# A hybrid encoder step in strassen form on one core: the first of the activations' sums, made by VectorE next to its second term

## The chip, the core and the metric

The kernel runs on one core of a Trainium2 chip. A core has five engines with a queue each: TensorE (PE; its weight loads are shown as PEld), VectorE (DVE), ScalarE (ACT), GpSimd (POOL) and SyncE (SP), which issues most transfers. Every engine takes its instructions in the order in which the program wrote them; between engines they wait on semaphores. The metric is the device time in microseconds (us) of one execution. All times here are of one profiled execution unless another source is named.

## The reference

One layer of an encoder runs over 2048 prompt frames and 64 frames of a running stream (17 tiles of 128 rows, the last of 64). What matters here is its second half:

```
def _post(x, mix, ln1_g, ln1_b, w_gate_up, w_down, ln2_g, ln2_b):
    h = _layernorm(ALPHA * x + mix, ln1_g, ln1_b)
    gu = h @ w_gate_up
    f = (jax.nn.silu(gu[..., :D_FF]) * gu[..., D_FF:]) @ w_down
    return _layernorm(ALPHA * h + f, ln2_g, ln2_b)
```

`h` has 1024 features, `D_FF` is 2816 = 22 slices of 128. Ahead of it stand a projection, a windowed attention, a gated mixer and an output projection, which take the first 600 us or so and are not touched.

## The kernel before

Numbers are float32. A product keeps that precision by splitting each operand into a rounded high part (`hi`, a cast by ACT) and the rest (`lo`, a subtraction by DVE, sometimes by POOL), and by three matmuls: hi·hi, hi·lo, lo·hi.

The second half goes over the tokens in four blocks (`b` = 0 to 3, of 576, 512, 512 and 512 tokens). In a block, each slice `i` of the 22 of gate and up is computed with Strassen's scheme in seven products (numbers 1 to 7) of 12 matmuls over 256 columns, in the order 1, [4 and 3 of the slice before], 5, 6, 2, 7. `product` issues one and then what evacuates its bank: ACT copies it into a buffer of the tag `tmp` (L915), DVE adds a bank to such a buffer (L919, L946), ACT takes the silu (L950, L958), and `out` multiplies gate by up (L926) into the activations `g`, with `sh` = 0 and 1 for the two halves of the block's tokens.

For two slices together (a pair `c` = slices 2c and 2c+1) the down projection is also done in seven products, in 23 pairs: c = 2 to 9 in blocks 1 and 2, and c = 2 to 8 in block 3 (`strassen`). The four quarters of the pair's activations are x = `g` of the even slice and y = `g` of the odd slice, each with the token halves 0 and 1. Products 1, 2 and 4 take x[0], y[0] and y[1] as they are (`put_f` splits them at once). Products 5, 6, 7 and 3 take sums: s5 = x[1] + y[1], s6 = s5 - x[0], s7 = x[0] - x[1], s3 = y[0] - s6. `f_sums` makes these four, `put_hi` casts one into a half of a buffer `ff` (L886) and `put_lo` subtracts (L890). `unit` does one down product for one tile of rows: three matmuls over 512 columns, hi·hi (L1333), hi·lo (L1334) and lo·hi (L1335, the only one that reads the lo part of the activations), and DVE adds the bank to `y` (L1338).

The order is written out by hand. The gate and up products of all blocks form one list; after the product at a position, what `todo` holds for this position is issued in the order in which it was entered. For a pair, p0 is the position of product 3 of its odd slice, where its last activations come out. Position p0+1 is product 5 of the next slice, p0+2 its 6, p0+3 its 2, p0+4 its 7, p0+5 product 1 of the slice after, p0+6 and p0+7 products 4 and 3. Units: 1 at p0 and p0+2, 2 at p0+1 and p0+3, 5 at p0+5 and p0+7, 6 at p0+6, and so on. The weights of the units are cast and subtracted by `split_hi` (L1322) and `split_lo` (L1326): those of product 5 at p0+2 and p0+3, those of 6 at p0+3 and p0+4. In blocks 1 and 2, POOL also makes eight differences of `h` for the next block (L747), at positions that fall into the pairs c = 3 and c = 5. The splits of the gate and up weights `wf` are shared by ACT (cast, L112) and DVE or POOL (subtraction, L113).

Of the kernel before, what the change touches and what calls it, by code (L numbers as in the profile page):

```python
# [11 lines left out]
ALU = mybir.AluOpType  # L12
# [33 lines left out]
def hybrid_step(ctx: ExitStack, tc: tile.TileContext, x_prompt, x_sample, xT_prompt, xT_sample, cache_kT, cache_v, w_in,  # L46
                ln_v_g, ln_v_b, sinks, w_spatialT, vecs, w_out, w_gate_up, w_down, ln2_g, ln2_b, rope,
                y_prompt, y_sample, wk_p, wv_p, nk_s, nv_s, nvm_s):
    nc = tc.nc
# [794 lines left out]
    ffs, spare, g_t, f_sum = {}, [], {}, {}  # L844
# [26 lines left out]
        f = ffs[b, c, prod] = half_form()  # L871
        split(f[:, 0], f[:, 1], src)

    def f_sums(b, c):

        x, y = g_t.pop((b, 2 * c)), g_t.pop((b, 2 * c + 1))
        for prod, o, a, d, op in ((5, y[:, 1], x[:, 1], y[:, 1], ALU.add), (7, x[:, 1], x[:, 0], x[:, 1], ALU.subtract),
                                  (6, x[:, 0], y[:, 1], x[:, 0], ALU.subtract), (3, y[:, 0], y[:, 0], x[:, 0], ALU.subtract)):
            nc.gpsimd.tensor_tensor(out=o, in0=a, in1=d, op=op)
        for prod, o in ((5, y[:, 1]), (6, x[:, 0]), (7, x[:, 1]), (3, y[:, 0])):  # L880
            f_sum[b, c, prod] = o

    def put_hi(b, c, prod):

# [12 lines left out]
    def product(b, i, prod):  # L897
        n = TB[b] // 2
        w, h = wf.pop((b, i, prod)), forms[b, prod]
        bk = {1: "A", 6: "A", 7: "A", 4: "A", 2: "B", 5: "C", 3: "C"}[prod]  # L900
        new = prod in (1, 2, 5)
        if new:
            acc[i, bk] = (bank({"A": f"A{i % 2}", "C": f"C{i % 2}", "B": "S1"}[bk]) if b else
                          ps1.tile([P, 512], F32, name=f"acc{bk}", tag="x", bufs=6))
        ps = acc[i, bk][:, :n]
        for k in range(4):
            wh, wl, hh, hl = w[:, 0, k], w[:, 1, k], h[:, 0, k, :n], h[:, 1, k, :n]

            nc.tensor.matmul(ps, wh, hh, start=(new and k == 0), stop=False, skip_group_check=not new)  # L909
            nc.tensor.matmul(ps, wh, hl, start=False, stop=False, skip_group_check=not new)  # L910
            nc.tensor.matmul(ps, wl, hh, start=False, stop=(k == 3), skip_group_check=not new)  # L911

        def keep(key):
            part[i, key] = tmp(key)
            nc.scalar.copy(part[i, key][:, :n], ps)  # L915

        def add(key, to):
            part[i, key] = a = part.pop((i, to))
            nc.vector.tensor_tensor(out=a[:, :n], in0=ps, in1=a[:, :n], op=ALU.add)  # L919

        def out(sh, g, u):
            if strassen(b, i):
                if sh == 0:
                    g_t[b, i] = f2.tile([P, 4, P], F32, name="g", tag="wsum", bufs=3).rearrange("p (s a) q -> p s (a q)", s=2)
                to = g_t[b, i][:, sh]
                nc.vector.tensor_tensor(out=to, in0=u, in1=g, op=ALU.mult)  # L926

                if not (sh and i % 2 == 0):
                    put_f(b, i // 2, 4 if sh else 1 + i % 2, to)
                if sh and i % 2:  # L930
                    f_sums(b, i // 2)
                return
            nc.vector.tensor_tensor(out=g, in0=u, in1=g, op=ALU.mult)
            f = ff[b, i][:, :, sh * n:(sh + 1) * n] if b == 0 else half_form()
            if b:
                ff[b, i, sh] = f
            split(f[:, 0], f[:, 1], g)

        if prod == 1:
            keep("a0")  # L940
        elif prod == 6:
            keep("a1")
        elif prod == 7:
            keep("a2")
            part[i, "c22"] = a = part.pop((i, "a2"))
            nc.vector.tensor_tensor(out=a[:, :n], in0=acc[i, "C"][:, :n], in1=a[:, :n], op=ALU.add)  # L946
        elif prod == 2:
            add("c11", "a0")
            g = part[i, "c11"][:, :n]
            nc.scalar.activation(g, g, AF.Silu)  # L950
        elif prod == 4:
            if b == 0:
                ff[b, i] = f2.tile([P, 4 * NHX], F32R, name="ff", tag="ff", bufs=4)[:, :4 * n].rearrange("p (s t) -> p s t", s=2)
            out(0, part.pop((i, "c11"))[:, :n], ps)
        elif prod == 3:
            add("c12", "a1")
            g = part.pop((i, "c12"))[:, :n]
            nc.scalar.activation(g, g, AF.Silu)  # L958
            out(1, g, part.pop((i, "c22"))[:, :n])
# [32 lines left out]
    for t in range(2, NP):  # L992
        a = t - 1
# [459 lines left out]
    for b in range(NB):  # L1453
        first, last = b * NO, b == NB - 1
        for c in range(NFF // 2):
            p0 = start[b, 2 * c + 1, 3]
            d_load, d_split = (-8, -1, -5, -3), (-3, 5, -1, 4)
            if strassen(b, 2 * c):
                for prod, q0, q1 in ((1, -6, -3), (2, -5, -2), (5, -2, 2), (6, -1, 3), (3, 1, 5), (7, 4, 7), (4, 6, 9)):
                    at(p0 + q0, lambda b=b, c=c, prod=prod: load_f(b, c, prod))  # L1460
                    at(p0 + q1, lambda b=b, c=c, prod=prod: split_hi(b, c, prod))
                    at(p0 + q1 + 1, lambda b=b, c=c, prod=prod: split_lo(b, c, prod))
                for q, prod, u in ((0, 1, 0), (1, 2, 0), (2, 1, 1), (3, 2, 1), (5, 5, 0), (6, 6, 0), (7, 5, 1), (8, 3, 0), (8, 6, 1),
                                   (9, 3, 1), (10, 7, 0), (11, 7, 1), (12, 4, 0), (13, 4, 1)):
                    at(p0 + q, lambda b=b, c=c, prod=prod, u=u: unit(b, c, prod, u))
                for q, prod in ((3, 5), (4, 6), (5, 3), (6, 7)):
                    at(p0 + q, lambda b=b, c=c, prod=prod: put_hi(b, c, prod))
                    at(p0 + q + 1, lambda b=b, c=c, prod=prod: put_lo(b, c, prod))
                continue
            if b == 0:  # L1470
                d_load, d_split = (-6, -2, 8, 0), (1, 0, 10, 3)
                for j, q0, q1 in ((0, 2, 4), (1, 4, 6), (2, 5, 7), (3, 11, 13)):
                    at(p0 + q0, lambda c=c, j=j: w_sum(c, j))
                    at(p0 + q1, lambda c=c, j=j: w_store(c, j))
            elif c == 0:
                d_load, d_split = (-5, 1, -3, 2), (0, 6, 3, 7)
            elif c == 1:
                d_load, d_split = (-8, -1, -4, 1), (-3, 5, 1, 6)
            elif c == NFF // 2 - 1 and not last:
                d_load, d_split = (0, 2, 1, 6), (5, 7, 6, 9)  # L1480
            elif last and c == NFF // 2 - 2:
                d_load, d_split = (-7, -5, -6, -2), (-4, -2, -3, 2)
            if last and c == NFF // 2 - 1:
                d_load, d_split = (-14, -11, -13, -8), (-11, -3, -4, -2)
            for h in range(2):
                for i in (2 * c, 2 * c + 1):
                    at(p0 + d_load[2 * (i % 2) + h], lambda b=b, i=i, h=h: load_d(b, i, h))
                    at(p0 + d_split[2 * (i % 2) + h], lambda b=b, i=i, h=h: split_d(b, i, h, b == NB - 1 and i > NFF - 3 and (i, h) != (NFF - 2, 0)))
            if c < NFF // 2 - (2 if last else 1):
                where = (5, 6, 7, 8, 9, 12, 13, 14, 15, 16) if b == 0 else (2, 4, 5, 7, 9, 10, 12, 13)  # L1490
                if c == 0 and b:
                    where = (10, 12, 14, 16, 17, 18, 19, 19) if b == 1 else (6, 10, 12, 14, 15, 16, 17, 18)
                for k, (h, t) in enumerate((h, t) for h in (range(2) if b else (1, 0)) for t in TILES[b]):
                    at(p0 + where[k], lambda b=b, c=c, t=t, h=h: down(b, c, t, h))
            elif not last:
                new = list(TILES[b + 1])
                if b:
                    at(p0 + 3, lambda t=new.pop(0): new_y(t))
                late = 0 if b else 2
                for k, t in enumerate(TILES[b]):  # L1500
                    for h in range(2):
                        at(p0 + 10 + 2 * k + (h if b else 2 - h), lambda b=b, c=c, t=t, h=h: down(b, c, t, h))
                    steps = finish_steps(t)
                    for q, f in zip((11, 12, 13, 15, 17), steps):
                        at(p0 + 2 * k + q + late, f)
                    at(p0 + 2 * k + 20 + late, lambda t=new.pop(0): new_y(t)) if new else None
        if not last:
            for pos, f in later_steps(b + 1):
                at(first + NO + pos, f)
    for pos in range(EARLY, len(order)):  # L1510
        b, i, p = order[pos]
# [102 lines left out]
```

## Time and profile before

| | |
|---|---|
| time, median of 3 runs | 2208.36 us (2204.99 to 2209.4) |
| the profiled execution's own time | 2207.18 us |
| its span, first to last instruction | 2205.4 us |
| mean granted TensorE clock | 0.987 of full speed |
| PE busy | 2089.7 us, 95% |
| DVE busy | 1640.3 us, 74% |
| ACT busy | 997.0 us, 45% |
| POOL busy | 702.2 us, 32% |

A profile of this kind has a page (engines, the span in slices, the chain of waits, groups of instructions) and views that are asked for: a list of who waited for whom, a timeline of one engine, and busy times by window. In a timeline a row gives the start, the duration, the engine, the source line, the operation, what it writes and reads with shapes, and in square brackets the idle time of the engine ahead of it with the instruction that ended it. Durations of neighbours on an engine overlap a little, since instructions are pipelined.

### The profile page before, as it was taken

To read this page: it belongs to the slowest core of one execution; us is meant where nothing else is said; L and a number is where in the kernel's file an instruction comes from. 1 tells how busy PE (TensorE), PEld (TensorE's weight loads), DVE (VectorE), ACT (ScalarE), POOL (GpSimd) and SP (SyncE) were. 2 spreads that over 40 slices of the span, in tenths; PEclk is the share of its full clock that TensorE was granted. 3 is DMA by queue.
4 is the path that set the end of the run, shared out by engine and by line. 5 is a ranking of instruction groups with operands and counts; after the bars stand their busy time and mean duration, and the time that the engine had idled before them with its cause. 6 is when DMAs were issued, how large, how long until landed. Compare 5 with 4: busy or idle time off the path is not lost.

```text
span 2205.4 us, 36220 instructions
## 1 busy us (share of the span) xinstructions
PE 2089.7 (95%) x13081; PEld 1861.6 (84%) x13081; DVE 1640.3 (74%) x3176; ACT 997.0 (45%) x2385; POOL 702.2 (32%) x644
## 2 busy tenths in 40 slices
PE   8999999989989899999999999999999999999997
PEld 6888888867768799999888888888888888988986
DVE  6877777786788677777786776777677778577775
ACT  6666666563343444444433443453343444344443
POOL 0222222231132567666531332222243222122221
PEclk9999999989999999999999999999999999999999
DMA  5111111043554866676776767787587777767663
GB/s 196 39 39 39 39 39 39 27 159 118 196 193 172 306 231 235 247 285 241 273 278 240 257 238 277 264 285 278 199 287 273 251 257 276 257 225 262 242 230 121
DMA packets 189156, 447.22 MB, mean 203 GB/s; under 512 B 22608, under 2 KB 53072, under 8 KB 188976
## 3 DMA queue, kind: packets, MB, share of 16 engines
q1 hardware_dynamic: 168432, 426.22, 54.9%
q10 hardware_dynamic: 20368, 18.35, 2.5%
q8 instruction: 103, 1.69, 0.3%
q14 instruction: 77, 0.63, 0.1%
q0 software_dynamic: 176, 0.33, 0.0%
HBM read 345.94 MB, written 98.89 MB: 202 GB/s over the span
## 4 chain that ended last, share of the span: by engine, by line
PE 65%; DVE 20%; ACT 6%; DMA 4%; issue 3%; POOL 1%; ACTq 0%; SPq 0%; DVEq 0%; POOLq 0%
PE bankA L909 5%; PE bankA L911 4%; PE bankA L910 4%; PE pj L158 2%; PE pj L159 2%; PE pj L160 2%; PE bankC L910 2%; PE bankC L909 2%; PE bankC L911 2%; PE pd L159 2%; PE pd L160 2%; PE pd L158 2%; PE bankD L1334 2%; PE bankD L1333 2%; PE bankD L1335 2%
## 5 line engine op out<-in xcount | busy, mean ns | idle before, releaser
L113 POOL TENSOR_TENSOR wf<-guraw,wf 128x512 fp32r<-128x512 f32 x173 | 245.7, 1420 | 626.9 <-ACT wf L112 598.4
L909 PE MATMUL bankA<-hf,wf 128*128 128x256 f32 x1056 | 301.8, 286 | 12.2 <-ACT a L915 11.9
L910 PE MATMUL bankA<-hf,wf 128*128 128x256 f32 x1056 | 300.1, 284 | 0.0
L911 PE MATMUL bankA<-hf,wf 128*128 128x256 f32 x1056 | 299.9, 284 | 0.0
L909 PEld LDWEIGHTS bankA<-hf,wf 128*128 128x128 f32 x1056 | 201.4, 191 | 22.7 <-ACT a L915 14.6
L910 PEld LDWEIGHTS bankA<-hf,wf 128*128 128x128 f32 x1056 | 201.2, 191 | 9.1
L911 PEld LDWEIGHTS bankA<-hf,wf 128*128 128x128 f32 x1056 | 201.4, 191 | 0.0
L112 ACT CAST wf<-guraw 128x512 fp32r<-128x512 f32 x264 | 163.1, 618 | 19.7 <-DMA guraw<-in_w_gate_up_dram 12.6
L915 ACT COPY a<-bankA 128x256 f32<-128x256 f32 x198 | 73.5, 371 | 174.8 <-PE bankA L911 174.4
L910 PE MATMUL bankC<-hf,wf 128*128 128x256 f32 x528 | 149.4, 283 | 2.6 <-DVE hf L113 2.6
L909 PE MATMUL bankC<-hf,wf 128*128 128x256 f32 x528 | 149.8, 284 | 0.9 <-DMA wf<-wf_d 0.8
L911 PE MATMUL bankC<-hf,wf 128*128 128x256 f32 x528 | 148.5, 281 | 0.0
L1338 DVE TENSOR_TENSOR y<-bankD,y 128x512 f32<-128x512 f32 x184 | 125.6, 683 | 30.5 <-PE bankD L1335 30.5
L1326 DVE TENSOR_TENSOR wd<-draw,wd 128x512 fp32r<-128x512 f32 x161 | 130.8, 813 | 0.0
L950 ACT ACTIVATE a<-a 128x256 f32<-128x256 f32 (+1 forms) x88 | 37.4, 425 | 200.7 <-DVE a L919 199.7
L909 PE MATMUL accA<-hf,wf 128*128 128x288 f32 x352 | 105.2, 299 | 8.9 <-ACT a L915 5.3
L958 ACT ACTIVATE a<-a 128x256 f32<-128x256 f32 (+1 forms) x88 | 37.4, 424 | 155.9 <-DVE a L919 155.8
L910 PEld LDWEIGHTS bankC<-hf,wf 128*128 128x128 f32 x528 | 99.5, 188 | 8.6 <-DVE hf L113 3.2
L1338 DVE TENSOR_TENSOR y<-bankS,y 128x512 f32<-128x512 f32 x138 | 94.4, 684 | 16.1 <-PE bankS L1335 13.7
L909 PEld LDWEIGHTS bankC<-hf,wf 128*128 128x128 f32 x528 | 99.8, 189 | 7.0 <-DMA wf<-wf_d 1.4
L911 PE MATMUL accA<-hf,wf 128*128 128x288 f32 x352 | 104.1, 296 | 0.4 <-DVE wf L113 0.4
L910 PE MATMUL accA<-hf,wf 128*128 128x288 f32 x352 | 104.4, 297 | 0.0
(336 smaller groups left out, 6712.1 us busy)
## 6 DMA issues: line engine op xcount, KB each, us to landing
wf<-wf_d SPq DMA_DIRECT2D x264, 512.0 KB, 4.9
guraw<-in_w_gate_up_dram SPq DMA_DIRECT2D x110, 512.0 KB, 6.2
wf_d<-wf SPq DMA_DIRECT2D x88, 512.0 KB, 4.9
draw<-in_w_down_dram SPq DMA_DIRECT2D x153, 256.0 KB, 3.5
draw<-wt_d SPq DMA_DIRECT2D x92, 256.0 KB, 4.3
guraw<-in_w_gate_up_dram SPq DMA_DIRECT2D x66, 256.0 KB, 6.4
wt_d<-draw SPq DMA_DIRECT2D x44, 256.0 KB, 3.3
hraw<-h_d SPq DMA_DIRECT2D x42, 256.0 KB, 4.7
```

Of the source, the lines that this page charges most:

```text
L112: nc.scalar.copy(hi, src)
L113: (on or nc.vector).tensor_tensor(out=lo, in0=src, in1=hi.bitcast(F32), op=ALU.subtract)
L158: nc.tensor.matmul(out, ah, bh, start=(i == 0), stop=False)
L159: nc.tensor.matmul(out, ah, bl, start=False, stop=False)
L160: nc.tensor.matmul(out, al, bh, start=False, stop=(i == n - 1))
L909: nc.tensor.matmul(ps, wh, hh, start=(new and k == 0), stop=False, skip_group_check=not new)
L910: nc.tensor.matmul(ps, wh, hl, start=False, stop=False, skip_group_check=not new)
L911: nc.tensor.matmul(ps, wl, hh, start=False, stop=(k == 3), skip_group_check=not new)
L915: nc.scalar.copy(part[i, key][:, :n], ps)
L1326: nc.vector.tensor_tensor(out=hl[:, 1], in0=d_raw.pop((b, c, "f", prod)), in1=hl[:, 0].bitcast(F32), op=ALU.subtract)
L1333: nc.tensor.matmul(pd, fh, w[:, 0], start=new, stop=False, skip_group_check=not new)
L1338: nc.vector.tensor_tensor(out=y, in0=pd, in1=y, op=ALU.add)
```

## The change

POOL makes three sums in place of four. The first, s5, is made by DVE directly behind the multiplication that gives y[1], and written into the buffer `u`, which held the up factor of that multiplication. POOL's s6 reads it there. Cast and subtraction of s5 are issued a product earlier: `put_hi` at p0+2 in place of p0+3, `put_lo` at p0+3 in place of p0+4. In the changed program the line numbers are shifted: 918 for 919, 925 for 926, 914 for 915, 948 for 946, 885 for 886, 889 for 890, 952 for 950, 1324 for 1322, 1328 for 1326, 1340 for 1338; the new addition is line 928.

```diff
-    def f_sums(b, c):
+    def f_sums(b, c, first):
 
         x, y = g_t.pop((b, 2 * c)), g_t.pop((b, 2 * c + 1))
-        for prod, o, a, d, op in ((5, y[:, 1], x[:, 1], y[:, 1], ALU.add), (7, x[:, 1], x[:, 0], x[:, 1], ALU.subtract),
-                                  (6, x[:, 0], y[:, 1], x[:, 0], ALU.subtract), (3, y[:, 0], y[:, 0], x[:, 0], ALU.subtract)):
-            nc.gpsimd.tensor_tensor(out=o, in0=a, in1=d, op=op)
-        for prod, o in ((5, y[:, 1]), (6, x[:, 0]), (7, x[:, 1]), (3, y[:, 0])):
+        for prod, o, a, d in ((7, x[:, 1], x[:, 0], x[:, 1]), (6, x[:, 0], first, x[:, 0]), (3, y[:, 0], y[:, 0], x[:, 0])):
+            nc.gpsimd.tensor_tensor(out=o, in0=a, in1=d, op=ALU.subtract)
             f_sum[b, c, prod] = o
+        f_sum[b, c, 5] = first
...
                 nc.vector.tensor_tensor(out=to, in0=u, in1=g, op=ALU.mult)
+                if sh and i % 2:
+
+                    nc.vector.tensor_tensor(out=u, in0=g_t[b, i - 1][:, 1], in1=to, op=ALU.add)
 
                 if not (sh and i % 2 == 0):
                     put_f(b, i // 2, 4 if sh else 1 + i % 2, to)
                 if sh and i % 2:
-                    f_sums(b, i // 2)
+                    f_sums(b, i // 2, u)
                 return
...
-                for q, prod in ((3, 5), (4, 6), (5, 3), (6, 7)):
+                for q, prod in ((2, 5), (4, 6), (5, 3), (6, 7)):
                     at(p0 + q, lambda b=b, c=c, prod=prod: put_hi(b, c, prod))
                     at(p0 + q + 1, lambda b=b, c=c, prod=prod: put_lo(b, c, prod))
```

The first place is VectorE at p0 of the second pair of block 1 (c = 3). `a1_13492` is the gate after its silu, `a2_13541` the up factor, `g_13594` the odd slice's activations, `g_13413` the even slice's. Before:

```order
L926 TENSOR_TENSOR g_13594<-a2_13541,a1_13492 128x256
L113 TENSOR_TENSOR ff_13596<-g_13594,ff_13596 128x256
L1338 TENSOR_TENSOR y_12732<-bankD0_12798,y_12732 128x512
L113 TENSOR_TENSOR wf_13638<-guraw_13351,wf_13638 128x512
L1338 TENSOR_TENSOR y_12732<-bankS0_12902,y_12732 128x512
```

and with the change:

```order
L925 TENSOR_TENSOR g_13594<-a2_13541,a1_13492 128x256
L928 TENSOR_TENSOR a2_13541<-g_13413,g_13594 128x256
L113 TENSOR_TENSOR ff_13596<-g_13594,ff_13596 128x256
L1340 TENSOR_TENSOR y_12732<-bankD0_12798,y_12732 128x512
L113 TENSOR_TENSOR wf_13638<-guraw_13352,wf_13638 128x512
```

The addition stands between the multiplication and the subtraction for product 4; nothing else moves there.

The second place is VectorE from p0+3 to p0+5 of the same pair. `wd` are the units' weights (of product 5, then of 6), `a2_13724` the next slice's up factor; the rows of line 890 are the subtractions for products 5 and 6. Before:

```order
L919 TENSOR_TENSOR a0_13565<-bankS1_12228,a0_13565 128x256
L1326 TENSOR_TENSOR wd_13675<-draw_13574,wd_13675 128x512
L1338 TENSOR_TENSOR y_12778<-bankS0_12902,y_12778 128x512
L946 TENSOR_TENSOR a2_13724<-bankC0_12168,a2_13724 128x256
L1326 TENSOR_TENSOR wd_13698<-draw_13604,wd_13698 128x512
L890 TENSOR_TENSOR ff_13704<-g_13594,ff_13704 128x256
L1338 TENSOR_TENSOR y_12829<-bankS1_12228,y_12829 128x512
L890 TENSOR_TENSOR ff_13704<-g_13413,ff_13704 128x256
```

and with the change:

```order
L918 TENSOR_TENSOR a0_13565<-bankS1_12228,a0_13565 128x256
L1328 TENSOR_TENSOR wd_13675<-draw_13574,wd_13675 128x512
L1340 TENSOR_TENSOR y_12778<-bankS0_12902,y_12778 128x512
L889 TENSOR_TENSOR ff_13681<-a2_13541,ff_13681 128x256
L948 TENSOR_TENSOR a2_13725<-bankC0_12168,a2_13725 128x256
L1328 TENSOR_TENSOR wd_13700<-draw_13604,wd_13700 128x512
L1340 TENSOR_TENSOR y_12829<-bankS1_12228,y_12829 128x512
L889 TENSOR_TENSOR ff_13681<-g_13413,ff_13681 128x256
```

The subtraction for product 5 has moved ahead of two instructions, the addition of the up factor and the subtraction of product 6's weights. On ScalarE its cast moved likewise, from behind the cast of product 6's weights to ahead of the silu of p0+3.

## Rows read from the trace of the kernel before

**Rows 1.** The page's first part, the row of TensorE: busy time, share of the span, instructions.

```profile
PE 2089.7 (95%) x13081; PEld 1861.6 (84%) x13081; DVE 1640.3 (74%) x3176; ACT 997.0 (45%) x2385; POOL 702.2 (32%) x644
```

**Rows 2.** The list of waits of TensorE from 1195 to 2150 us, the stretch that holds the 23 pairs: who waited for whom, us in total, times, the longest.

```profile
PE bankS L1335 <- DVE ff L890: 25.3, 23, 2.2
PE bankS L909 <- DVE y L1338: 7.7, 6, 2.3
PE bankA L909 <- ACT a L915: 6.7, 3, 2.8
```

**Rows 3.** Timeline of TensorE at p0+5 and p0+6 of a pair of block 3 (c = 4), and the same wait one pair later.

```profile
2004.32 0.40 PE L1334 MATMUL bankS<-wd,ff 128*128 128x512 f32 x1
2005.77 0.50 PE L1335 MATMUL bankS<-wd,ff 128*128 128x512 f32 x1 [1.05 <-DVE ff L890]
2006.10 0.28 PE L909 MATMUL bankA<-hf,wf 128*128 128x256 f32 x1
...
2007.76 0.39 PE L1334 MATMUL bankD<-wd,ff 128*128 128x512 f32 x1
2007.99 0.40 PE L1335 MATMUL bankD<-wd,ff 128*128 128x512 f32 x1
...
2036.82 0.50 PE L1335 MATMUL bankS<-wd,ff 128*128 128x512 f32 x1 [1.05 <-DVE ff L890]
```

**Rows 4.** Timeline of VectorE in this pair, from the multiplication at p0 to the subtraction for product 6 at p0+5.

```profile
1996.35 0.43 DVE L926 TENSOR_TENSOR g<-a,a 128x256 f32<-128x256 f32 x1 [0.48 <-ACT a L958]
1997.25 0.43 DVE L113 TENSOR_TENSOR ff<-g,ff 128x256 fp32r<-128x256 f32 x1 [0.47 <-ACT ff L112]
1997.59 0.68 DVE L1338 TENSOR_TENSOR y<-bankD,y 128x512 f32<-128x512 f32 x1
1998.19 0.85 DVE L113 TENSOR_TENSOR wf<-guraw,wf 128x512 fp32r<-128x512 f32 x1
...
2000.74 0.42 DVE L919 TENSOR_TENSOR a<-bankS,a 128x256 f32<-128x256 f32 x1 [0.50 <-PE bankS L911]
2001.08 0.74 DVE L1326 TENSOR_TENSOR wd<-draw,wd 128x512 fp32r<-128x512 f32 x1
2001.75 0.68 DVE L1338 TENSOR_TENSOR y<-bankS,y 128x512 f32<-128x512 f32 x1
2003.27 0.42 DVE L946 TENSOR_TENSOR a<-bankC,a 128x256 f32<-128x256 f32 x1 [0.84 <-ACT a L915]
2003.61 0.68 DVE L1326 TENSOR_TENSOR wd<-draw,wd 128x512 fp32r<-128x512 f32 x1
2004.21 1.50 DVE L890 TENSOR_TENSOR ff<-g,ff 128x256 fp32r<-128x256 f32 x1
2006.30 0.69 DVE L1338 TENSOR_TENSOR y<-bankS,y 128x512 f32<-128x512 f32 x1 [0.59 <-PE bankS L1335]
2006.91 0.41 DVE L890 TENSOR_TENSOR ff<-g,ff 128x256 fp32r<-128x256 f32 x1
```

**Rows 5.** Timeline of GpSimd in this pair: the four sums, then a split of gate and up weights.

```profile
1997.76 3.52 POOL L879 TENSOR_TENSOR g<-g 128x256 f32<-128x256 f32 x4 [2.77 <-DVE ff L113]
2004.14 1.29 POOL L113 TENSOR_TENSOR wf<-guraw,wf 128x512 fp32r<-128x512 f32 x1 [2.86 <-ACT wf L112]
```

**Rows 6.** Timeline of ScalarE in this pair: the cast of product 5's weights, the silu of p0+3, the cast of s5, the copy at p0+4, the cast of s6, the cast that releases GpSimd's split.

```profile
1998.88 0.62 ACT L1322 CAST wd<-draw 128x512 fp32r<-128x512 f32 x1
2001.20 0.42 ACT L950 ACTIVATE a<-a 128x256 f32<-128x256 f32 x1 [1.69 <-DVE a L919]
...
2002.03 0.41 ACT L886 CAST ff<-g 128x256 fp32r<-128x256 f32 x1
2002.87 0.37 ACT L915 COPY a<-bankA 128x256 f32<-128x256 f32 x1 [0.43 <-PE bankA L911]
2003.13 0.41 ACT L886 CAST ff<-g 128x256 fp32r<-128x256 f32 x1
2003.44 0.62 ACT L112 CAST wf<-guraw 128x512 fp32r<-128x512 f32 x1
```

**Rows 7.** The raw gate and up weights of a slice: their issue on SP's queue in this pair (two transfers), the median time from issue to landing of the larger in the stretch 1990 to 2025 us, and the cast by ScalarE that reads them at p0+7.

```profile
1999.02 0.86 SPq L805 DMA_DIRECT2D guraw<-in_w_gate_up_dram  x2
...
guraw<-in_w_gate_up_dram SPq DMA_DIRECT2D x2, 512.0 KB, 6.2
...
2008.81 0.62 ACT L112 CAST wf<-guraw 128x512 fp32r<-128x512 f32 x1
```

**Rows 8.** Pair c = 3 of block 1, timelines of GpSimd, VectorE and TensorE: the second difference of `h`, the subtraction for product 6, and the matmul that reads it.

```profile
1256.62 1.48 POOL L747 TENSOR_TENSOR hsum<-hraw,hsum 128x512 f32<-128x512 f32 x1
...
1258.16 0.41 DVE L890 TENSOR_TENSOR ff<-g,ff 128x256 fp32r<-128x256 f32 x1
...
1259.26 0.40 PE L1335 MATMUL bankD<-wd,ff 128*128 128x512 f32 x1
```

**Rows 9.** Pairs c = 5 of blocks 1 and 2: ScalarE and TensorE waiting for transfers in block 1, the wait of block 2 in TensorE's timeline, and a window of block 2 behind it (busy us and instructions of PE, PEld, DVE, ACT and POOL, granted clock, DMA share, GB/s).

```profile
1322.59 0.62 ACT L1322 CAST wd<-draw 128x512 fp32r<-128x512 f32 x1 [3.79 <-DMA draw<-in_w_down_dram]
1323.85 0.39 PE L909 MATMUL bankC<-hf,wf 128*128 128x256 f32 x1 [0.78 <-DMA wf<-wf_d]
...
1681.46 0.50 PE L1335 MATMUL bankS<-wd,ff 128*128 128x512 f32 x1 [2.16 <-DVE ff L890]
...
1682.00:1685.00 3.00, 3.00 (x14) 2.90 (x14) 1.44 (x3) 0.21 (x2) 0.55 (x1) 0.50 1.04 421
```

## The prediction

> **What bounds the kernel now.** I read the page's engine row first: TensorE is busy for 95% of the span [rows 1], so only TensorE's idle time can be won, and the next view is the list of who ended it. In the stretch of the 23 pairs that list has one large entry: 25.3 us, 23 times, once in every pair. In each, the third matmul of a unit (L1335) waits for the subtraction that makes the lo part of a sum (L890). The next two entries, 7.7 and 6.7 us, have 9 waits between them [rows 2]. The timeline of TensorE gives the place: unit 5 at p0+5. Its second matmul starts at 2004.32, its third at 2005.77, and the next product's first at 2006.10 [rows 3]. At the pace of the next unit (second matmul at 2007.76, third at 2007.99, 0.23 us apart) the third would have started at 2004.55 or so and the next product 0.23 us behind it. The wait therefore moves everything behind it by 2006.10 - 2004.78 = 1.32 us, a little more than the 1.05 us of idle time in the list. It returns after 2036.82 - 2005.77 = 31.05 us, in the next pair [rows 3].
>
> Why the subtraction is late is in VectorE's timeline [rows 4]. At p0+4 it stands third: the addition of the up factor, which itself waits 0.84 us for ScalarE's copy, then the subtraction of product 6's weights, then the one for s5. That takes 1.50 us in place of the 0.41 us that the next one of its kind takes. GpSimd's split runs from 2004.14 to 2005.43 [rows 5], and VectorE's instruction, begun at 2004.21, ends at 2005.71, 0.28 us behind it. So two things delay TensorE: a place in the queue, and a collision with GpSimd at that place.
>
> **The move of cast and subtraction.** With the change the subtraction for s5 stands directly behind the addition to `y` that ends at 2001.75 + 0.68 = 2002.43, and in front of the addition at 2003.27. VectorE is idle there for 0.84 us [rows 4], the subtraction takes 0.41 us, and GpSimd has nothing between 2001.28 (1997.76 + 3.52) and 2004.14 [rows 5]. It ends near 2002.85, 1.7 us ahead of the 2004.55 at which TensorE wants it. The addition and the weights' subtraction behind it stay where they were, since their start is set by ScalarE's copy at 2002.87 [rows 6]; so the weights' subtraction still begins at 2003.61, ahead of GpSimd's split. The cast moves on ScalarE to behind the cast of 1998.88, which ends at 1999.50; ScalarE then has 1.69 us of idle time before the silu [rows 6], and the cast takes 0.41 us. Cost: nothing; without this cover it would delay the silu by at most 0.41 us.
>
> **The new addition.** 23 additions of 128x256 on VectorE at the 0.43 us of the multiplication beside them are 9.9 us of work. Each falls into the 0.47 us in which VectorE waits for the cast for product 4 anyway [rows 4]: the multiplication ends at 1996.78, the addition would end near 1997.25, and the subtraction behind it starts at 1997.25 now. I take 0. The bounds are 0 and, uncovered and passed on to TensorE in full, 9.9 us; a gain is excluded, since an instruction is added to that queue. Nearest to 0, because VectorE also idles 0.50 us at 2000.74 [rows 4].
>
> **What leaves GpSimd.** One of four sums goes, 3.52 / 4 = 0.88 us per pair, and the other three start at the addition's end (about 1997.3) instead of 1997.76, so the chain ends near 1997.3 + 2.64 = 1999.9 instead of 2001.28 [rows 5]. Nothing waits for it at the old time: the cast of s6 at 2003.13 stands behind ScalarE's copy of 2002.87 [rows 6]. Gain 0. The earlier start puts the sums beside the subtraction of 1997.25 and the `wf` subtraction of 1998.19, which may each lose up to one sum, 0.88 us. The idle 0.50 and 0.84 us behind them take up 1.34 us; I count nothing and keep 0.4 us per pair, 9 us, as the upper bound.
>
> *By the Trainium skill, page "SBUF — State Buffer", section "Who interferes with whom", a VectorE instruction with two SBUF inputs and a GpSimd instruction that reads SBUF block each other for the whole instruction, and the one issued first wins. The 1.50 us row agrees. By that rule the new addition is itself such an instruction, and it lets GpSimd go at the moment at which the subtraction for product 4 wants to start; this is the mechanism of the last rival below.*
>
> **What is late next.** TensorE's work behind p0+5 starts 1.32 us earlier, and what follows TensorE (copies, additions to `y`, products) follows it. Two things do not. The subtraction for s6 must be done for the third matmul of unit 6, now 2007.99, then 2006.67. It is behind the addition to `y` of unit 5, which moves from 2006.30 to 2004.98 and ends at 2005.67; GpSimd's split has ended at 2005.43; so the subtraction ends near 2006.05, with 0.6 us to spare. The raw weights are issued at 1999.02, land 6.2 us later at 2005.2, and are cast at 2008.81, then 2007.49 [rows 7]: 2.3 us to spare.
>
> **The sum.** 19 of the 23 pairs look like this one: 19 x 1.32 = 25.1 us. In the two pairs c = 3 GpSimd goes on from its split with a difference of `h`, 1256.62 to 1258.10. The subtraction for s6, now 1258.16, would be wanted by 1259.26 - 1.32 = 1257.94, but by the 0.28 us seen above it ends at 1258.38 [rows 8]. A wait of about 0.45 us, with 0.1 us of restart, stays: 2 x 0.75 = 1.5 us gained. In c = 5 of block 1 ScalarE waits 3.79 us and TensorE 0.78 us for transfers right behind [rows 9]; what is won is waited for there: 0. In c = 5 of block 2 the wait is 2.16 us, and behind it the granted clock is 0.50, TensorE's level of 1.2 GHz, for a window of 3 us, while transfers fill the queues (DMA share 1.04) [rows 9]. If all goes it is worth 1.32 + 1.11 + 1.5 = 3.9 us, if the transfers set the pace 0; I take 1.5. Together 25.1 + 1.5 + 0 + 1.5 = 28.1 us off the profiled execution's own 2207.18, which is 2179.1. The median shown is 1.2 us above that execution, so 2180.3; forecast 2180.
>
> **Rivals.** *The wait moves to unit 6.* If VectorE loses a race with GpSimd's split at p0+4 in ordinary pairs too, s6 is late as in c = 3: 0.75 instead of 1.32 us in each, 21 x 0.75 + 1.5 = 17.3 us, so 2191. For it: only 0.53 us lie between the weights' subtraction (2003.61) and the split (2004.14). Against: both are released by ScalarE's copies and keep their order.
>
> *The change does not reach TensorE.* The new cast could wait, for a half of an `ff` buffer or for the sum, or the transfers could give the saved time back everywhere. Then 2208. For it: c = 5. Against: ScalarE's 1.69 us, and 2.3 us of margin for the raw weights.
>
> *Slower: GpSimd wins at p0.* GpSimd's three sums start just as VectorE wants the subtraction for product 4. If GpSimd is first each time, four VectorE subtractions with both inputs in SBUF (product 4, `wf`, product 5's weights, s5) can each wait for a sum of 0.88 us: 3.5 us. The idle 0.47 (used by the addition), 0.50 and 0.84 us take 1.34 of it, and 2.2 us reach the additions that free banks S0 and S1. A wait of that length had the clock at 0.50 behind it in c = 5 [rows 9], worth 1.5 us more. It decides once the new wait passes 1.32 us; at 2.2 alone each pair loses 0.9 us and the time is 2208 + 19 = 2227. Against: three sums last 2.6 us and cannot meet four instructions spread over 5 us.
>
> **How the numbers follow.** Forecast 0.75, its own range 2175 to 2186: all of c = 5 won gives 2176, the addition half uncovered 2185. The wait at unit 6: 0.13. No effect: 0.06. Slower: 0.06. A difference under 0.2%, 4.4 us, could not be told from none, so faster 0.88, same 0.06, slower 0.06. The range for 8 in 10 reaches from 2174 to the second case with a little room for runs: 2194.
>
> **What would show it.** Right: the 23 waits for the subtraction of a sum at unit 5 are gone from TensorE's list, the period of ordinary pairs is 29.7 instead of 31.05 us, the subtraction for s5 takes 0.41 us, and VectorE's subtraction for product 4 still starts 0.9 us behind the multiplication. In the c = 3 pairs a short wait appears at unit 6. Wrong: waits at the third matmul of unit 6 in every pair, waits for additions to `y` at p0+3, or transfers ahead of the casts of raw weights.

## The result, and the profile after

The changed kernel is faster. The ratio of its time to that of the kernel before is 0.9872, with a 95% interval of 0.9844 to 0.9900; a second lot of runs of the same kernel gives 0.9863 (0.9849 to 0.9877). The median is 2181.45 us in the first lot (2178.54 us without one disturbed run of its four, which the ratio leaves out) and 2177.35 us in the second, against 2208.51 and 2207.32 us before. Forecast were 2180 us and a range of 2174 to 2194. The profiled execution took 2175.76 us, 31.4 us less than the one before.

The first view is again the list of waits of TensorE, from 1195 to 2150 us (the third matmul of a unit is now L1337, the first of a product L908).

```profile
PE bankS L908 <- DVE y L1340: 8.9, 7, 2.3
PE bankA L908 <- ACT a L914: 6.8, 5, 2.8
PE bankC L909 <- DVE hf L113: 2.1, 2, 1.0
PE bankD L1337 <- DVE ff L889: 1.7, 4, 0.7
PE bankS L1335 <- DVE y L1340: 0.4, 1, 0.4
```

The entry of 25.3 us and 23 times that led [rows 2] is gone. The entries for additions to `y` and ScalarE's copies, 7.7 and 6.7 us before, are 8.9 and 6.8. One entry has grown, from one wait to four: those at unit 6 (bank D, for the subtraction of s6), two of 0.19 us in the pairs c = 3 and two of 0.67 us in c = 5. Before it was this line:

```profile
PE bankD L1335 <- DVE ff L890: 0.3, 1, 0.3
```

The page's first row shows the same work in a shorter span, with one more VectorE and one fewer GpSimd instruction per pair:

```profile
PE 2082.2 (96%) x13081; PEld 1860.9 (86%) x13081; DVE 1624.5 (75%) x3199; ACT 997.5 (46%) x2385; POOL 691.3 (32%) x621
```

The timeline of TensorE at p0+5 of the pair of rows 3 (c = 4 of block 3):

```profile
1979.54 0.40 PE L1336 MATMUL bankS<-wd,ff 128*128 128x512 f32 x1
1979.77 0.39 PE L1337 MATMUL bankS<-wd,ff 128*128 128x512 f32 x1
1980.00 0.28 PE L908 MATMUL bankA<-hf,wf 128*128 128x256 f32 x1
```

Third matmul and next product follow at 0.23 us each; before, they came 1.45 and 0.33 us behind their neighbours [rows 3]. VectorE in this pair, the counterpart of [rows 4]:

```profile
1971.58 0.42 DVE L925 TENSOR_TENSOR g<-a,a 128x256 f32<-128x256 f32 x1 [0.48 <-ACT a L960]
1972.04 0.43 DVE L928 TENSOR_TENSOR a<-g 128x256 f32<-128x256 f32 x1
1972.48 0.43 DVE L113 TENSOR_TENSOR ff<-g,ff 128x256 fp32r<-128x256 f32 x1
...
1976.90 0.69 DVE L1340 TENSOR_TENSOR y<-bankS,y 128x512 f32<-128x512 f32 x1
1977.50 0.42 DVE L889 TENSOR_TENSOR ff<-a,ff 128x256 fp32r<-128x256 f32 x1
1978.49 0.42 DVE L948 TENSOR_TENSOR a<-bankC,a 128x256 f32<-128x256 f32 x1 [0.57 <-ACT a L914]
1978.83 0.68 DVE L1328 TENSOR_TENSOR wd<-draw,wd 128x512 fp32r<-128x512 f32 x1
1980.20 0.69 DVE L1340 TENSOR_TENSOR y<-bankS,y 128x512 f32<-128x512 f32 x1 [0.68 <-PE bankS L1337]
1980.81 0.41 DVE L889 TENSOR_TENSOR ff<-g,ff 128x256 fp32r<-128x256 f32 x1
```

The new addition (L928) runs from 1972.04 to 1972.47. The subtraction for product 4 starts at 1972.48, 0.90 us behind the multiplication, as before (1996.35 to 1997.25). The subtraction for s5 (L889) takes 0.42 us where it took 1.50, and ends at 1977.92, 1.85 us ahead of the matmul that reads it. GpSimd, the counterpart of [rows 5]:

```profile
1972.55 0.96 POOL L878 TENSOR_TENSOR g<-g 128x256 f32<-128x256 f32 x1 [2.33 <-DVE a L928]
1973.58 1.12 POOL L878 TENSOR_TENSOR g<-a,g 128x256 f32<-128x256 f32 x1
1974.78 0.74 POOL L878 TENSOR_TENSOR g<-g 128x256 f32<-128x256 f32 x1
1979.36 1.30 POOL L113 TENSOR_TENSOR wf<-guraw,wf 128x512 fp32r<-128x512 f32 x1 [3.84 <-ACT wf L112]
```

GpSimd's first sum starts 0.07 us behind VectorE's subtraction and takes 0.96 us, the second 1.12, the third, alone, 0.74. It is GpSimd that gives way at p0.

How the gain is spread shows when the starts of the multiplication at p0 (L926 before, L925 after) are taken from both timelines for all 23 pairs. Each line is the time from this multiplication in one pair to the one in the next, so it holds the wait at unit 5 of the pair named (20 such times, since the last pair of a block has none behind it):

```
pair                            before    after   changed kernel again (e4)
block 1, c = 2                   31.80    30.45    30.46
block 1, c = 3                   31.73    30.84    31.13
block 1, c = 4                   31.01    28.99    29.51
block 1, c = 5                   37.31    34.27    36.35
block 1, c = 6, 7, 8 (mean)      31.11    29.77    29.77
block 2, c = 2                   31.80    30.51    30.50
block 2, c = 3                   31.69    30.80    30.84
block 2, c = 4                   30.32    29.00    28.98
block 2, c = 5                   34.51    33.19    34.95
block 2, c = 6, 7, 8 (mean)      31.08    29.78    29.76
block 3, c = 2                   31.82    30.48    30.46
block 3, c = 3 to 7 (mean)       31.07    29.77    29.77
```

An ordinary pair loses 1.3 us, every time. The c = 3 pairs lose 0.89, and c = 4 and c = 5 are not alike from one execution to the next.

### The profile page after: what moved, and what is told of

The parts are those of the page before. It is cut to its first block, busy times and chain, and to the rows that moved or that the text cites. A ratio compares the mean times of both kernels' runs of the same rounds, so it can differ in the third digit from the quotient of the medians.

```text
span 2174.0 us, 36223 instructions
## 1 busy us (share of the span) xinstructions
PE 2082.2 (96%) x13081; PEld 1860.9 (86%) x13081; DVE 1624.5 (75%) x3199; ACT 997.5 (46%) x2385; POOL 691.3 (32%) x621
## 4 chain that ended last, share of the span: by engine, by line
PE 67%; DVE 19%; ACT 5%; DMA 4%; issue 3%; POOL 1%; SPq 0%; ACTq 0%; DVEq 0%; POOLq 0%
PE bankA L908 5%; PE bankA L909 5%; PE bankA L910 5%; PE pj L158 2%; PE pj L159 2%; PE pj L160 2%; PE bankC L909 2%; PE bankC L908 2%; PE bankC L910 2%; PE pd L159 2%; PE pd L160 2%; PE pd L158 2%; PE po L158 2%; PE po L160 2%; PE po L159 2%
## 5 line engine op out<-in xcount | busy, mean ns | idle before, releaser
L908 PE MATMUL bankA<-hf,wf 128*128 128x256 f32 x1056 | 301.5, 285 | 11.6 <-ACT a L914 11.5
L908 PEld LDWEIGHTS bankA<-hf,wf 128*128 128x128 f32 x1056 | 201.4, 191 | 23.4 <-ACT a L914 14.2
L908 PE MATMUL bankC<-hf,wf 128*128 128x256 f32 x528 | 149.4, 283 | 0.2
L908 PE MATMUL accA<-hf,wf 128*128 128x288 f32 x352 | 105.1, 299 | 8.9 <-ACT a L914 5.3
L908 PEld LDWEIGHTS bankC<-hf,wf 128*128 128x128 f32 x528 | 99.6, 189 | 5.7 <-ACT hf L112 0.5
```

## The experiments

Eleven kernels, in three lots. "Before" in a ratio is the kernel before, run on the same chip.

**e1, e2 and e3: which part of the change does it.** In e1 only the place changes; GpSimd makes all four sums as before:

```diff
-                for q, prod in ((3, 5), (4, 6), (5, 3), (6, 7)):
+                for q, prod in ((2, 5), (4, 6), (5, 3), (6, 7)):
```

> Only the place is changed: GpSimd still makes all four sums, cast and subtraction of s5 are issued a product earlier. Theory A (the place of the subtraction on VectorE is what counts, because the old place collides with GpSimd's split): GpSimd's first sum ends near 1998.5 in the pair of rows 4 to 6, a microsecond before ScalarE reaches the cast, so the 23 waits at unit 5 go as they do in the changed kernel; about 25 to 28 us faster than before, 2181 us, and some 2 to 4 us slower than the changed kernel, in the pairs c = 4 and c = 5 where GpSimd's chain is long. Theory B (the sum must be made by VectorE to be there in time): ScalarE waits for GpSimd, the waits at unit 5 stay at about 1 us, 2205 us or more.

Measured: ratio 0.9883 (0.9865 to 0.9900), median 2182.41 us. The waits at unit 5 are gone. VectorE's and ScalarE's rows in c = 4 of block 3:

```profile
1984.51 0.41 DVE L890 TENSOR_TENSOR ff<-g,ff 128x256 fp32r<-128x256 f32 x1
...
1981.57 0.41 ACT L886 CAST ff<-g 128x256 fp32r<-128x256 f32 x1
```

ScalarE casts the sum of GpSimd at once behind the weights' cast, without idle time, and the subtraction takes 0.41 us. Theory B falls: GpSimd's s5 is there in time. The 2 to 4 us that e1 was expected to lie behind the changed kernel can't be told from these ratios (0.9883 against 0.9872 and 0.9863, with intervals that overlap); e10 below settles it.

e2 is the opposite: VectorE makes the sum, cast and subtraction stay at p0+3 and p0+4 (the change without the line above).

> Only the maker is changed: VectorE makes s5, cast and subtraction stay at p0+3 and p0+4. Theory A: the subtraction still stands behind the weights' subtraction and meets GpSimd's split, so the 23 waits of 1.05 us stay; only the shorter chain of GpSimd can show, at most 4 us in the pairs c = 4 and c = 5; 2204 us (2202 to 2208). Theory B: the waits go, 2180 us.

Measured: ratio 0.9983 (0.9973 to 0.9994), median 2205.54 us. Its list of waits of TensorE from 1190 to 2150 us and its timeline of VectorE in block 3:

```profile
PE bankS L1337 <- DVE ff L889: 25.7, 23, 2.1
...
2002.32 1.50 DVE L889 TENSOR_TENSOR ff<-a,ff 128x256 fp32r<-128x256 f32 x1
```

All 23 waits are there, and the subtraction takes 1.50 us again, although its operand had been ready for 7.0 us (the addition ran from 1994.92 to 1995.34). The sum by VectorE alone gives 0.17%, some 4 us; its pairs c = 4 and c = 5 of block 1 took 30.31 and 33.99 us.

e3 leaves the sums and the casts as in the kernel before and exchanges two neighbours on VectorE at p0+4:

```diff
+                at(p0 + 4, lambda b=b, c=c: put_lo(b, c, 5))
                 for prod, q0, q1 in ((1, -6, -3), (2, -5, -2), (5, -2, 2), (6, -1, 3), (3, 1, 5), (7, 4, 7), (4, 6, 9)):
...
-                    at(p0 + q + 1, lambda b=b, c=c, prod=prod: put_lo(b, c, prod))
+                    if prod != 5:
+                        at(p0 + q + 1, lambda b=b, c=c, prod=prod: put_lo(b, c, prod))
```

> Before, with one exchange on VectorE at p0+4: the subtraction for s5 ahead of the subtraction of product 6's weights, all else as before. Theory A: the subtraction begins at 2003.6, half a microsecond ahead of GpSimd's split, takes 0.42 us and ends before TensorE wants it (2004.55): the waits go, about 25 us faster than before, 2182 us. If instead the length of VectorE's queue up to p0+4 were the cause, and not the collision, this moves the subtraction by 0.6 us only and about 0.7 us of each wait stays: 2197 us. A third outcome: the weights' subtraction now meets the split, and a wait of about 0.5 us appears at unit 6 in each pair: 2193 us.

Measured: ratio 0.9869 (0.9854 to 0.9884), median 2179.72 us: all of the gain. VectorE and GpSimd at p0+4 in block 3:

```profile
1983.16 0.42 DVE L890 TENSOR_TENSOR ff<-g,ff 128x256 fp32r<-128x256 f32 x1
1983.49 0.68 DVE L1326 TENSOR_TENSOR wd<-draw,wd 128x512 fp32r<-128x512 f32 x1
...
1983.69 1.65 POOL L113 TENSOR_TENSOR wf<-guraw,wf 128x512 fp32r<-128x512 f32 x1 [2.86 <-ACT wf L112]
```

The subtraction for s5 starts one instruction, some 0.6 us, sooner than in the order before and is done some 1.7 us sooner, because it no longer meets GpSimd's split. The weights' subtraction behind it is under way before the split starts, so VectorE loses nothing (0.68 us) and GpSimd takes 1.65 us instead of 1.29. A wait of 1.05 us that goes with a move of 0.6 us was a collision, not a long queue: at its old start, 2004.21, a subtraction of 0.42 us would have ended at 2004.63, 0.08 us behind the 2004.55 at which TensorE wanted it. The third outcome did not come either. In ordinary pairs the list has no wait for a subtraction; four short ones are left in the pairs c = 5, two at unit 5 (1.0 us in all) and two at unit 6 (1.5 us).

**e4: the changed kernel again.**

> The changed kernel once more, to see what repeats. If the gains per pair are the program's own, each ordinary pair again takes 29.8 us and the pairs c = 4 and c = 5 of block 1 together again about 63.3 us (28.99 + 34.27); if the 5 us won in those two pairs were an accident of the transfers, they move by some microseconds.

Measured: ratio 0.9863 (0.9849 to 0.9877). The profiled execution took 2181.13 us, 5.4 us more than the first one. The ordinary pairs are the same to 0.03 us (table above); c = 4 and c = 5 of block 1 take 65.86 us together instead of 63.26, and c = 5 of block 2 34.95 instead of 33.19. So the 5 us that the first profile showed as won in c = 4 and c = 5 of block 1 were half an accident. Most of what differs is TensorE's clock. In both pairs c = 5 of e4 there is a stretch with a granted clock near 0.50, the level of 1.2 GHz, and in the first profile of the changed kernel there is none. The windows of busy time (columns as in [rows 9]), first e4, then the first profile:

```profile
1332.00:1335.00 3.00, 3.00 (x15) 2.71 (x14) 1.71 (x3) 0.42 (x1) 0.00 (x0) 0.54 0.98 287
1680.00:1683.00 3.00, 2.95 (x14) 2.86 (x15) 1.53 (x3) 0.00 (x0) 0.00 (x0) 0.56 0.88 299
```
```profile
1330.00:1333.00 3.00, 3.00 (x22) 2.80 (x22) 1.86 (x4) 0.61 (x2) 0.00 (x0) 1.00 0.96 349
1676.00:1679.00 3.00, 3.00 (x24) 2.86 (x24) 2.52 (x5) 0.42 (x1) 0.00 (x0) 1.00 0.94 292
```

Added up over the pair, what the granted clock lacks of 1.00 comes to 1.7 us in each of the two pairs of e4 (an estimate from windows of 1 us). Without it they take 34.65 and 33.24 us, against 34.27 and 33.19.

**e5: the price of the addition.** The new line stands twice in the changed kernel:

```diff
                     nc.vector.tensor_tensor(out=u, in0=g_t[b, i - 1][:, 1], in1=to, op=ALU.add)
+                    nc.vector.tensor_tensor(out=u, in0=g_t[b, i - 1][:, 1], in1=to, op=ALU.add)
```

> The changed kernel with the new addition made twice (the second writes the same values again): 23 more instructions of 0.43 us on VectorE, not covered by the wait for ScalarE's cast, which the first one fills. Theory A (VectorE has slack at p0, 0.66 us of idle time before the bank of p0+3): no pair becomes longer, 2178 us as the changed kernel (2176 to 2182). Rival (VectorE is the bound next to TensorE, so each instruction more is paid): 23 x 0.43 = 9.9 us more, 2188 us.

Measured: ratio 0.9868 (0.9851 to 0.9884), median 2178.00 us, and 29.77 us for the ordinary pairs. VectorE in c = 4 of block 3:

```profile
1976.22 0.43 DVE L928 TENSOR_TENSOR a<-g 128x256 f32<-128x256 f32 x1
1976.69 0.42 DVE L929 TENSOR_TENSOR a<-g 128x256 f32<-128x256 f32 x1
1977.03 0.41 DVE L113 TENSOR_TENSOR ff<-g,ff 128x256 fp32r<-128x256 f32 x1
```

The second addition delays the subtraction for product 4 by 0.36 us, to 1.26 us behind the multiplication of 1975.77, and no ordinary pair pays for it. The idle time of VectorE ahead of p0+3 shrinks by the same 0.36 us, from 0.66 in the changed kernel to 0.30 in e5:

```profile
1975.96 0.42 DVE L918 TENSOR_TENSOR a<-bankS,a 128x256 f32<-128x256 f32 x1 [0.66 <-PE bankS L910]
```
```profile
1980.15 0.42 DVE L918 TENSOR_TENSOR a<-bankS,a 128x256 f32<-128x256 f32 x1 [0.30 <-PE bankS L910]
```

**e6: GpSimd's fourth sum put back.** The changed kernel with one more addition on GpSimd, whose result nobody uses:

```diff
+        nc.gpsimd.tensor_tensor(out=y[:, 1], in0=x[:, 1], in1=y[:, 1], op=ALU.add)
         for prod, o, a, d in ((7, x[:, 1], x[:, 0], x[:, 1]), (6, x[:, 0], first, x[:, 0]), (3, y[:, 0], y[:, 0], x[:, 0])):
```

> The changed kernel, but GpSimd also makes its old first addition (into the place where it stood, read by nobody), so its chain is as long as before. Theory A (GpSimd's shorter chain is worth nothing in ordinary pairs): ordinary pairs stay at 29.8 us; only c = 4 and c = 5 may grow, by up to 4 us together; 2178 to 2183 us. Rival (part of the gain comes from work taken off GpSimd): ordinary pairs grow by some tenths, 2185 us or more.

Measured: ratio 0.9876 (0.9861 to 0.9891), median 2180.02 us; ordinary pairs 29.77 us; c = 4 and c = 5 of block 1 29.00 and 34.74. Within what these pairs vary by, the fourth sum costs nothing that can be told.

**e7 and e8: what makes c = 5 long.** In e7 the loads, differences and stores for the next block move to other positions:

```diff
-            q = -100 + 24 * kk
+            q = -96 + 28 * kk
```

> The changed kernel with the differences of h for the next block (loads, subtractions on GpSimd, stores) put 4 positions later for the first half and 8 later for the second, so that they fall to p0+8 to p0+14 of the pairs c = 3 and c = 5. If the short waits left at unit 6 come from these subtractions, the c = 3 pairs go from 30.8 to 30.4 us and the waits at unit 6 go: 1 to 2 us, and up to 4 more if SP's queue is held for a shorter time in c = 5: 2173 to 2178 us. If not, no change in c = 3.

A miss: ratio 0.9902 (0.9886 to 0.9917), median 2185.63 us, slower than the changed kernel. The waits at unit 6 are gone from its list, but c = 3 takes 30.70 us in block 1, only 0.1 less, and 30.98 in block 2, 0.2 more. The pairs c = 5 fall to 31.05 and 31.36 us, and the pairs behind c = 3 and c = 5 become 31.73 and 32.38 us long in block 1 (31.70 and 33.52 in block 2). The waits moved with what was moved, to the additions to `y`: 12.4 us in 11 waits instead of 8.9 in 7.

e8 moves only the stores, 5 positions behind their subtractions:

```diff
             nc.gpsimd.tensor_tensor(out=t[out, kk], in0=t[x, kk], in1=t[y, kk], op=ALU.subtract)
+
+        def store(out, kk, prod):
             nc.sync.dma_start(out=hs_d[b][prod][:, 2 * kk:2 * kk + 2], in_=t[out, kk])
...
             yield q + 12, lambda kk=kk: sub("b21", "b21", "t2", kk, 4)
+            for d, out, prod in ((6, "t1", 5), (8, "t2", 6), (10, "b12", 7), (12, "b21", 4)):
+                yield q + d + 5, lambda kk=kk, out=out, prod=prod: store(out, kk, prod)
```

> The changed kernel with each store of such a difference issued 5 positions after its subtraction, so that SP's queue does not stand before it. If the long c = 5 pairs (34 to 36 us in block 1, 33 to 35 in block 2) come from SP waiting for GpSimd, with the loads of weights queued behind, they fall to 30 to 31 us and the whole to about 2170 us; if they come from the amount of transfers at that place, they stay and so does the time, 2178 us.

Measured: ratio 0.9841 (0.9826 to 0.9855), median 2171.95 us. c = 5 takes 30.64 us in block 1 and 30.20 in block 2. What it removes is in the list of waits of SP's queue, which issues the loads, and in that queue's timeline. In the kernel before, 1306 to 1326 us, c = 5 of block 1:

```profile
SPq L748 <- POOL hsum L747: 11.6, 2, 11.3
...
1306.20 0.32 SPq L1316 DMA_DIRECT2D draw<-wt_d  x1
1317.91 0.32 SPq L748 DMA_DIRECT2D hs_d<-hsum  x1
1318.33 0.37 SPq L1316 DMA_DIRECT2D draw<-in_w_down_dram  x1
1318.80 0.40 SPq L833 DMA_DIRECT2D wf<-wf_d  x1
```

For 11.3 us SP stands before one store, whose data GpSimd has yet to subtract, and the loads of weights stand behind it. The changed kernel has the same entry at 8.5 us, e8 none. The windows of busy time show what the transfers do meanwhile (columns as in [rows 9], behind the length of the stretch), before, in the changed kernel and in e8:

```profile
1310.00:1322.00 12.00, 10.95 (x79) 9.91 (x77) 9.83 (x14) 4.93 (x12) 10.36 (x9) 1.00 0.26 59
```
```profile
1306.00:1318.00 12.00, 12.00 (x88) 11.06 (x86) 10.31 (x17) 5.63 (x14) 10.84 (x9) 1.00 0.46 120
```
```profile
1306.00:1318.00 12.00, 12.00 (x89) 11.30 (x88) 10.26 (x17) 6.29 (x15) 10.45 (x9) 1.00 0.94 328
```

They are busy for 0.26 of the time before, for 0.46 in the changed kernel and for 0.94 in e8.

**e9, e10 and e11: the same late stores with the kernel before, with e1 and with e3.**

> The kernel before with the stores of the differences issued 5 positions later, nothing else. The 23 waits of 1.05 us at unit 5 stay; only c = 5 of blocks 1 and 2 (37.3 and 34.5 us) fall, to about 31.9 and 31.5: some 8 us less than before, 2199 us. If the gain of the late stores needs the changed sums, nothing: 2207 us.

> As e1 (GpSimd makes all four sums, cast and subtraction a product earlier), with the late stores, so that the pairs c = 5, which differ from run to run, no longer blur the comparison. Theory A (who makes s5 counts for nothing): 2172 us as e8 within 2 us. If the sum by VectorE is worth something by itself: 2174 us or more.

> As e3 (one exchange on VectorE at p0+4, sums by GpSimd at their old place), with the late stores. Theory A: 2172 us within 2 us, as e8 and e10; a smaller gain would say that the earlier cast and the new sum add something to leaving the collision.

Measured: e9 0.9974 (0.9965 to 0.9983), median 2200.63 us, with all 23 waits and c = 5 at 32.97 and 33.08 us, 1.1 and 1.6 more than expected; e10 0.9845 (0.9832 to 0.9858), 2171.92 us; e11 0.9847 (0.9833 to 0.9861), 2172.72 us. e8, e10 and e11 agree within 0.8 us. With SP's long wait in c = 5 out of the way, it makes no difference who adds s5 or by how much its subtraction moves, as long as it leaves the collision; and the two gains add up: 0.26% for the stores (e9) and 1.31% for the subtraction (e3) make 1.57%, where e11, with both, has 1.53%. By the ratios each of the three is 0.25 to 0.31%, some 6 us, better than the changed kernel in its first lot and 0.16 to 0.22%, some 4 us, better than in its second, whose interval they overlap.

## Why the prediction was right

**The wait and its price.** The step "19 x 1.32 = 25.1 us" holds: the ordinary pairs lose 1.29 to 1.35 us each. That 1.32 and not the 1.05 us of the list is the price is right too, and so is the cause, place and collision: e2 keeps the place and the wait, e3 gives up the collision and loses the wait.

**The new addition at 0.** Right: e5 makes a second one without loss. The cover is not the 0.47 us of the cast alone but the idle time on VectorE ahead of p0+3 as well, which the prediction named as a second reserve.

**What is late next.** Unit 6 in the c = 3 pairs, as forecast, with 0.19 us of wait instead of 0.45, and 0.89 us won instead of 0.75 (0.60 and 0.85 in e4). The rows of c = 3 in block 1, the counterpart of [rows 8]:

```profile
1256.08 1.29 POOL L747 TENSOR_TENSOR hsum<-hraw,hsum 128x512 f32<-128x512 f32 x1
...
1256.26 1.39 DVE L889 TENSOR_TENSOR ff<-g,ff 128x256 fp32r<-128x256 f32 x1
...
1257.70 0.50 PE L1337 MATMUL bankD<-wd,ff 128*128 128x512 f32 x1 [0.19 <-DVE ff L889]
```

GpSimd's difference runs from 1256.08 to 1257.37, and the subtraction ends at 1257.65, again 0.28 us behind it. By the first profile the term was 0.14 us per pair too small. In e3 the order of the two is the other one, since GpSimd's split ahead of them is longer there (1.64 us in this pair):

```profile
1258.51 0.48 DVE L890 TENSOR_TENSOR ff<-g,ff 128x256 fp32r<-128x256 f32 x1
...
1258.68 1.47 POOL L747 TENSOR_TENSOR hsum<-hraw,hsum 128x512 f32<-128x512 f32 x1
```

There the pairs c = 3 have no wait at unit 6 and take 30.42 and 30.40 us: all of the 1.3 us is won. The prediction did not have the waits of 0.67 us at unit 6 in c = 5.

**The pairs c = 5: the step that failed.** "What is won is waited for there: 0" took the transfers as the pace in block 1, whatever the engines do. The transfers were nearly idle just ahead (0.26). What held them was SP's queue, standing before a store that waits for GpSimd; e8 shows it by moving that store. In the first profile block 1 won 2.02 us in c = 4 and 3.04 in c = 5 where 1.32 and 0 were counted, and block 2's c = 5 1.32 where 1.5 was; in e4 it was 1.50, 0.96 and -0.44. Both pairs c = 5 of the kernel before hold a stretch of lower clock, 1.7 us each by the same estimate as for e4, which the first profile of the changed kernel happens not to hold. Without these stretches c = 5 of block 1 won 1.3 us (1.0 in e4), and c = 5 of block 2 nothing in either profile (-0.4). So the 1.5 that was counted for block 2 is near 1.32 by luck. By the first profile the sum was 3.3 us too small (31.4 against 28.1), by e4's 2.0 too large (2207.18 - 2181.13 = 26.1). The same step stands behind "nothing waits for it at the old time" in the part on GpSimd: in c = 5 SP does. Its longest wait there in block 1 is 8.5 us in the changed kernel (9.0 in e4) and 9.4 with the fourth sum put back, although e6 could not find a price for that.

**The rivals.** The wait did not move to unit 6 in ordinary pairs: the weights' subtraction starts at 1978.83, the split at 1979.36, still 0.53 us apart. The slower case did not come, for a reason that the prediction did not give: at p0 VectorE's subtraction is ready 0.07 us ahead of GpSimd's first sum, and GpSimd pays, 0.96 and 1.12 us for sums that take 0.74 alone. By the Trainium skill, page "SBUF — State Buffer", section "Who interferes with whom", the first to issue keeps the port and the other waits; the traces agree in both directions, VectorE waiting (1.50 us, c = 3 above) and GpSimd waiting (1.65 us in e3). In size GpSimd's wait is a little under the whole overlap: in e3 its split starts 0.48 us ahead of the end of VectorE's instruction and takes 0.36 us longer.

**The clock.** The window of granted clock 0.50 behind the wait of 2.16 us [rows 9] is gone in the first profile of the changed kernel, whose windows from 1652 to 1688 us have 1.00. But c = 5 of block 2 did not gain the 3.9 us that this allowed, since a wait of 1.18 us for an addition to `y` and one of 0.67 us at unit 6 came in its place. Nor did the window go for good: e4 has it again (0.56, shown under e4), behind waits of 0.79 and 1.17 us for additions to `y`. Block 1 had such a window before the change too, behind a wait of 1.94 us, which the prediction did not see:

```profile
1334.00:1337.00 3.00, 2.89 (x13) 2.89 (x14) 1.35 (x3) 0.13 (x1) 0.00 (x0) 0.50 0.72 220
```

In the changed kernel's first profile a wait of 1.89 us at the same place has a granted clock of 1.00 behind it. So the removed wait at unit 5 does not by itself give the clock back, and what decides between the two is not shown.

## What to carry to other kernels

When an instruction takes far longer than its equals (here 1.50 against 0.42 us), look at what the other user of its port does at that moment before moving work between engines: exchanging two neighbours in an in-order queue won all that the larger change won. Price a wait by how far the work behind it moves, not by the idle time in a list. And in a queue that issues transfers, an entry that waits for a computation holds every load behind it; low transfer activity just ahead of a wait for transfers is the sign.

## What had not been expected

One store held SP's queue for 11.3 us, and moving the stores won 0.26%, some 6 us, in the kernel before (e9). Whether it also makes the time steadier is not shown: the five runs of e8 lie between 2171.19 and 2172.53 us, the four of e4 between 2176.62 and 2181.13, but those of e10 between 2169.70 and 2174.77. The profiles say more. With the stores at their old place some executions hold a stretch of lower clock in c = 5 (before, e1, e2, e4) and others do not (the changed kernel's first, e3, e5, e6); in none of the four with late stores (e8 to e11) does c = 5 hold one. That is one profile of each.
